# Buffers and banks for two units of a gated recurrence, and its low weight parts on VectorE

## The chip, the cores and the metric

One core of a Trainium2 chip runs the whole program. The metric is device time in microseconds (us); the kernel before was run three times, and one more execution was recorded with the hardware profiler. TensorE is called PE here, VectorE DVE, ScalarE ACT, GpSimd POOL and SyncE SP, as in the profile; PEld is the loading of weights into PE.

## The reference

The trunk has two layers on 1024 tokens of width 1024. The first layer mixes tokens with a gated linear recurrence (HGRN2), the second with latent attention; a causal convolution MLP follows each. The change is in the recurrence alone:

```python
def _hgrn2_mixer(h, w_in, lower_bound, out_norm, w_out):
    q, f, i, g = jnp.split(h @ w_in, 4, axis=-1)
    forget = lb + (1.0 - lb) * jax.nn.sigmoid(f)
    key_in = 1.0 - forget
    log_f = jnp.log(forget)
    o = _chunk_gated_recurrence(heads(jax.nn.silu(q)), heads(key_in), heads(i), heads(log_f))
    o = _rmsnorm(o, out_norm) * jax.nn.silu(heads(g))
    return o.reshape(B, S, D_MODEL) @ w_out
# S_t = diag(f_t) S_{t-1} + k_t v_t^T ;  o_t = S_t^T q_t   per head, 8 heads, key and value width 128
```

## The kernel before

Every product is made from fp32 data that is split into a high part (rounded by ACT, line 128, the tile `whi` or `vgh`) and a low part (what is left, a subtraction, line 131, the tile `wlo` or `vgl`). PE multiplies high by high, high by low and low by high (`acc3`, lines 147 to 149).

`hgrn` works in 16 units, one for each of 8 heads and each of two halves (`hf`) of 512 tokens. Each unit has two parts.

- `project` makes the forget gate `Fg` with the key `K` (line 364 on), the query `q` and its gated form `Q` (lines 373 to 376), each from 24 matmuls of 512 columns into a bank `ps_mm`; then the value `v` and the output gate `g` from 96 matmuls of 256 columns (tiles `vgh`, `vgl`).
- `recur` makes the decayed scores by doubling: a group of 8 small matmuls (line 406, tile `sc`) gives the scores of one level, then DVE scales half of `Q` (line 417) and POOL half of `K` (line 419) with running decays `tot` (line 422), and the next level follows; one group with `q`, six levels, then line 432. After them come the transposed key (`pT`, line 443, copied by ACT at line 445), the state updates (`pu`, line 456; line 461 on DVE), the output `po` (lines 451 and 453) and its norm (lines 465 to 471). `flip` transposes the finished output (line 478), splits it and sends it out.

`weights` fetches the four weight tiles of a head into a ring of two raw tiles and splits them. A head's set is made while an earlier head is still running. The last units are taken in the order (6,0), (7,0), (6,1), (7,1), so that weights are made ten times, four tiles each. After the units, `out_projection` multiplies all heads' outputs (`oall`), 192 matmuls for each half.

The code names one tile after another; a scheduler in the framework puts each engine's instructions in order ahead of time, by data, buffers (`bufs`) and banks. At run time each engine takes its own list strictly in that order. A tile with one buffer can't be written again before its last reader is done; a PSUM bank likewise. So the number of buffers decides how early the scheduler can place the work of a following unit.

Of the kernel before, what the change touches and what calls it, by code (L numbers as in the profile page):

```python
# [9 lines left out]
F32 = mybir.dt.float32  # L10
# [9 lines left out]
P = 128  # L20
D = 1024
S = 1024
HF = 512
# [7 lines left out]
LEVELS = (1, 2, 4, 8, 16, 32)  # L31
# [27 lines left out]
def trunk_kernel(ctx: ExitStack, tc: tile.TileContext, x, pos, par, gout, cst, msk, w_hin, w_hout,  # L59
                 w_min, w_qup, w_kvup, w_mout, w_up, w_down, out):  # L60
    nc = tc.nc
    pe, dve, act, pool = nc.tensor, nc.vector, nc.scalar, nc.gpsimd
# [6 lines left out]
    psg = ctx.enter_context(tc.tile_pool(name="psg", bufs=2, space=PSUM))  # L69
# [18 lines left out]
    def fetch_w(src):  # L88
        raw = wpool.tile([P, 1024], F32, tag="wraw", name="wraw", bufs=2)
        nc.sync.dma_start(out=raw, in_=src)  # L90
        return raw
# [41 lines left out]
    def load_w(src, tag="w", wp=None, bufs=3, eng=pool):  # L133
        lo_eng = dve if first else eng
        raw = first.pop(0) if first else fetch_w(src)
        hi = (wp or wpool).tile([P, 1024], F32R, tag=tag + "hi", name="whi", bufs=bufs)
        lo = (wp or wpool).tile([P, 1024], F32R, tag=tag + "lo", name="wlo", bufs=bufs)
        split(raw, hi, lo, lo_eng=lo_eng)
        return hi, lo

    def v3(ap, a):
        return ap.rearrange("p (a b) -> p a b", a=a)
# [178 lines left out]
    def hgrn(layer, h):  # L321
        with ExitStack() as st:
            tp = st.enter_context(tc.tile_pool(name="g_t", bufs=2))
            early = st.enter_context(tc.tile_pool(name="g_e", bufs=2))
            wv = st.enter_context(tc.tile_pool(name="g_wv", bufs=1))
            ps = st.enter_context(tc.tile_pool(name="g_ps", bufs=1, space=PSUM))
# [11 lines left out]
            wts = {}  # L338

            def weights(hd):  # L340
                wf = load_w(w_hin[8 + hd])
                wq = load_w(w_hin[hd])
                vgh = wv.tile([P, KD, 2 * P], F32R, tag="vgh", name="vgh")
                vgl = wv.tile([P, KD, 2 * P], F32R, tag="vgl", name="vgl")
                for i, src in enumerate((w_hin[16 + hd], w_hin[24 + hd])):
                    raw = vg_first.pop(0) if vg_first else fetch_w(src)
                    split(v3(raw, KD), vgh[:, :, i * P:(i + 1) * P], vgl[:, :, i * P:(i + 1) * P],
                          lo_eng=dve if vg_first else pool)
                wts[hd] = wf, wq, vgh, vgl

            def project(hd, hf, bank=ps_mm):
                wf, wq, vgh, vgl = wts[hd]
                hh, hl, rb, y = h[hf]

                def proj(w):
                    p = bank()
                    acc3(p, [(w[0][:, k * P:(k + 1) * P], w[1][:, k * P:(k + 1) * P], hh[:, k, :], hl[:, k, :])
                             for k in range(KD)])
                    return p

                pf = proj(wf)
                Fg = early.tile([P, HF], F32, tag="F", name="Fg")
                K = tp.tile([P, HF], F32, tag="K", name="K")
                dve.tensor_tensor(out=Fg, in0=pf, in1=rb, op=ALU.mult)
                act.activation(out=K, in_=Fg, func=AF.Sigmoid, scale=-1.0)
                act.activation(out=Fg, in_=Fg, func=AF.Sigmoid)
                pool.tensor_scalar(out=Fg, in0=Fg, scalar1=oml[:, hd:hd + 1], scalar2=lb[:, hd:hd + 1],
                                   op0=ALU.mult, op1=ALU.add)
                pool.tensor_scalar(out=K, in0=K, scalar1=oml[:, hd:hd + 1], scalar2=0.0, op0=ALU.mult, op1=ALU.add)
                pq = proj(wq)  # L370
                q = early.tile([P, HF], F32, tag="q", name="q", bufs=1)
                Q = tp.tile([P, HF], F32, tag="Q", name="Q")
                dve.tensor_tensor(out=q, in0=pq, in1=rb, op=ALU.mult)  # L373
                act.activation(out=Q, in_=q, func=AF.Sigmoid)
                dve.tensor_tensor(out=q, in0=q, in1=Q, op=ALU.mult)
                dve.tensor_tensor(out=Q, in0=q, in1=Fg, op=ALU.mult)

                v = tp.tile([P, 4, P], F32, tag="v", name="v")
                g = tp.tile([P, 4, P], F32, tag="g", name="g", bufs=3)
                for tt in range(2):  # L380
                    pv = ps_mm()
                    for t2 in range(2):
                        t = 2 * tt + t2
                        ts_ = slice(t * P, (t + 1) * P)
                        acc3(pv[:, t2 * 256:(t2 + 1) * 256],
                             [(hh[:, k, ts_], hl[:, k, ts_], vgh[:, k, :], vgl[:, k, :]) for k in range(KD)])
                    p3 = v3(pv, 2)
                    for t2 in range(2):
                        t = 2 * tt + t2
                        yt = y[:, t:t + 1]  # L390
                        act.activation(out=v[:, t, :], in_=p3[:, t2, 0:P], func=AF.Identity, scale=yt)
                        act.activation(out=g[:, t, :], in_=p3[:, t2, P:2 * P], func=AF.Sigmoid, scale=yt)
                        dve.scalar_tensor_tensor(out=g[:, t, :], in0=p3[:, t2, P:2 * P], scalar=yt, in1=g[:, t, :],  # L393
                                                 op0=ALU.mult, op1=ALU.mult)
                pool.tensor_tensor(out=g, in0=g, in1=goutb[:, None, :].broadcast_to([P, 4, P]), op=ALU.mult)
                return Fg, K, q, Q, v, g

            def recur(hd, hf, prj, state):
                Fg, K, q, Q, v, g = prj

                def scores(qq):
                    sc = ps.tile([P, 4, 64], F32, tag="sc", name="sc", bufs=2)
                    for c in range(4):
                        for b in range(2):
                            sl = slice(c * P + b * 64, c * P + b * 64 + 64)
                            pe.matmul(sc[b * 64:b * 64 + 64, c, :], lhsT=K[:, sl], rhs=qq[:, sl], start=True, stop=True)  # L406
                    return sc

                SD = tp.tile([P, 4, 64], F32, tag="SD", name="SD", bufs=1)
                dve.tensor_tensor(out=SD, in0=scores(q), in1=fold[:, None, 0:64].broadcast_to([P, 4, 64]), op=ALU.mult)  # L410

                def scale(tot, m):
                    nb = HF // (2 * m)
                    tv = tot.rearrange("p (b two) -> p b two", two=2)
                    Qv = Q.rearrange("p (b two m) -> p b two m", two=2, m=m)
                    Kv = K.rearrange("p (b two m) -> p b two m", two=2, m=m)
                    dve.tensor_tensor(out=Qv[:, :, 1, :], in0=Qv[:, :, 1, :],  # L417
                                      in1=tv[:, :, 0:1].broadcast_to([P, nb, m]), op=ALU.mult)
                    pool.tensor_tensor(out=Kv[:, :, 0, :], in0=Kv[:, :, 0, :],
                                       in1=tv[:, :, 1:2].broadcast_to([P, nb, m]), op=ALU.mult)  # L420
                    nt = tp.tile([P, nb], F32, tag=f"tot{m}", name=f"tot{m}", bufs=2 if m == 64 else 1)
                    dve.tensor_tensor(out=nt, in0=tv[:, :, 0], in1=tv[:, :, 1], op=ALU.mult)
                    return nt

                tot = Fg
                for li, m in enumerate(LEVELS):
                    sc = scores(Q)
                    tot = scale(tot, m)
                    dve.copy_predicated(SD, masks[:, li, None, :].broadcast_to([P, 4, 64]), sc)
                sc = ps.tile([P, 4, 64], F32, tag="sc", name="sc64", bufs=2)  # L430
                for c in range(4):
                    pe.matmul(sc[0:64, c, :], lhsT=K[:, c * P:c * P + 64], rhs=Q[:, c * P + 64:(c + 1) * P],
                              start=True, stop=True)
                ST = tp.tile([P, 4, P], F32, tag="ST", name="ST", bufs=1)
                pool.memset(ST[64:P, :, 0:64], 0.0)
                act.copy(out=ST[0:64, :, 0:64], in_=SD[0:64])
                act.copy(out=ST[64:P, :, 64:P], in_=SD[64:P])
                act.copy(out=ST[0:64, :, 64:P], in_=sc[0:64])
                tot = scale(tot, 64)
# [9 lines left out]
                for c in range(4):  # L449
                    first = state is None  # L450
                    pe.matmul(po[:, c, :], lhsT=ST[:, c, :], rhs=v[:, c, :], start=True, stop=first)
                    if not first:
# [33 lines left out]
            vg_first = []  # L486
# [6 lines left out]
            goutb = wv.tile([P, P], F32, tag="goutb", name="goutb")  # L493
            nc.sync.dma_start(out=goutb, in_=gout.partition_broadcast(P))
            nc.sync.dma_start(out=cs, in_=cst)
            mstage = tp.tile([P, len(LEVELS), 64], F32, tag="ST", name="mstage", bufs=1)
            nc.sync.dma_start(out=mstage, in_=msk)
            dve.tensor_copy(out=masks, in_=mstage)
            prj = project(0, 0, ps_wo)
# [549 lines left out]
```

## Time and profile before

| what | us |
|---|---|
| median of three runs | 2585.41 |
| lowest and highest of them | 2581.57, 2588.17 |
| the profiled execution | 2581.05 |
| its span, first to last instruction | 2579.2 |

The span is 1.85 us shorter than the profiled execution's own time. A row of a timeline gives the start, the duration, the engine, the line, the operation, the tiles as written<-read, and, in brackets, how long the engine had stood idle before it and who ended that. Durations of matmuls overlap, since they are pipelined: the difference between two starts tells what one costs.

### The profile page before, as it was taken

The numbers are of one execution on the slowest core, as the hardware profiler recorded it, in microseconds if no ns is written. First come the engines' busy times: TensorE is split into PE (matmuls) and PEld (weight loads), VectorE is DVE, ScalarE is ACT, GpSimd is POOL, SyncE is SP. The second block draws the span as 40 slices with busy tenths as digits, with TensorE's granted clock in tenths as the row PEclk, the third lists the DMA queues.
The fourth block names the chain that finished last, engine by engine and source line by source line (L and its number), as shares of the span: only waits on it lengthen the run. The fifth ranks groups of instructions, "written<-read, shape, count | busy, mean of one in ns | idle before, by whom it ended". The sixth has DMA issues, their size and how long they took to land.

```text
span 2579.2 us, 35799 instructions
## 1 busy us (share of the span) xinstructions
PE 2483.0 (96%) x13860; PEld 2069.2 (80%) x13860; DVE 1698.1 (66%) x3033; ACT 1080.6 (42%) x1777; POOL 392.5 (15%) x386
## 2 busy tenths in 40 slices
PE   7999999998999999999999999999999999999999
PEld 6888888876777778888888788888877787888887
DVE  8355555555788888774535777777578888875333
ACT  5322223322444444433433566656444444443322
POOL 3334445521100000000003323221000000000000
PEclk9999999999999999999999999989999999999999
DMA  3111111343433332264331000002543333226443
GB/s 138 42 50 50 50 50 66 113 144 121 154 120 111 108 112 89 90 230 155 128 126 50 17 34 33 34 26 103 200 155 120 109 110 111 91 91 220 155 170 116
DMA packets 88298, 270.18 MB, mean 105 GB/s; under 512 B 9920, under 2 KB 10304, under 8 KB 86976
## 3 DMA queue, kind: packets, MB, share of 16 engines
q1 hardware_dynamic: 88128, 267.90, 29.5%
q8 instruction: 109, 1.79, 0.3%
q14 instruction: 61, 0.50, 0.1%
HBM read 207.04 MB, written 60.82 MB: 104 GB/s over the span
## 4 chain that ended last, share of the span: by engine, by line
PE 86%; DVE 6%; ACT 3%; DMA 3%; issue 1%; SPq 0%; ACTq 0%; DVEq 0%
PE ps_mm L251 19%; PE ps_up L251 9%; PE ps_mm L147 8%; PE ps_mm L149 8%; PE ps_mm L148 7%; PE ps_up L942 7%; PE ps_mm L942 5%; PE ps_wo L942 5%; PE ps_wo L251 3%; PE sp L710 3%; PE ps_misc L942 2%; PE sc L406 2%; PE ps_misc L167 2%; DMA open_spill<-part 1%; PE ps_wo L739 1%
## 5 line engine op out<-in xcount | busy, mean ns | idle before, releaser
L128 ACT CAST whi<-wraw 128x1024 fp32r<-128x1024 f32 (+1 forms) x328 | 321.3, 993 | 579.2 <-PE ps_misc L942 236.6
L131 DVE TENSOR_TENSOR wlo<-wraw,whi 128x1024 fp32r<-128x1024 f32 (+1 forms) x298 | 337.9, 1146 | 286.3 <-ACT whi L128 285.9
L251 PE MATMUL ps_mm<-bop,whi 128*128 128x512 f32 x1536 | 477.7, 393 | 17.3 <-ACT x L888 9.5
L251 PEld LDWEIGHTS ps_mm<-bop,whi 128*128 128x128 f32 x1536 | 285.9, 188 | 89.8 <-ACT x L888 15.4
L251 PE MATMUL ps_mm<-bop,wlo 128*128 128x512 f32 x768 | 296.4, 391 | 0.9 <-DVE wlo L131 0.9
L862 DVE SCALAR_TENSOR_TENSOR x<-x,prm,x 128x1023 f32<-128x1023 f32 (+1 forms) x176 | 223.5, 1279 | 48.9 <-ACT x L859 47.9
L251 PE MATMUL ps_up<-bop,whi 128*128 128x512 f32 x704 | 220.7, 394 | 0.9 <-ACT whi L128 0.9
L251 PEld LDWEIGHTS ps_mm<-bop,wlo 128*128 128x128 f32 x768 | 144.2, 188 | 33.6 <-DVE wlo L131 2.2
L942 PE MATMUL ps_up<-ring,whi 128*128 128x512 f32 x528 | 159.9, 389 | 0.0
L251 PEld LDWEIGHTS ps_up<-bop,whi 128*128 128x128 f32 x704 | 131.8, 188 | 33.1 <-ACT whi L128 2.6
L417 DVE TENSOR_TENSOR Q<-Q,tot 128x256 f32<-128x256 f32 x96 | 65.6, 683 | 133.2 <-PE sc L406 105.3
L147 PE MATMUL ps_mm<-vgh,hh 128*128 128x256 f32 x512 | 146.0, 285 | 5.9 <-DVE q L373 5.6
L149 PE MATMUL ps_mm<-vgh,hl 128*128 128x256 f32 x512 | 145.4, 284 | 0.0
L148 PE MATMUL ps_mm<-vgl,hh 128*128 128x256 f32 x512 | 143.8, 281 | 0.0
L859 ACT ACTIVATE x<-x,prm 128x1024 f32<-128x1024 f32 x88 | 109.3, 1243 | 70.0 <-DVE x L886 48.2
L251 PE MATMUL ps_up<-bop,wlo 128*128 128x512 f32 x352 | 138.5, 394 | 0.0
L845 DVE TENSOR_TENSOR wraw<-wraw 128x512 f32<-128x512 f32 x176 | 120.8, 686 | 2.2
L147 PE MATMUL ps_mm<-hh,whi 128*128 128x512 f32 x288 | 115.7, 402 | 2.2 <-DVE g L393 1.2
L710 PE MATMUL sp<-kk,qq 128*128 128x256 f32 (+4 forms) x480 | 109.1, 363 | 8.7 <-ACT pp L725 8.5
L942 PEld LDWEIGHTS ps_up<-ring,whi 128*128 128x128 f32 x528 | 99.2, 188 | 20.7
L149 PE MATMUL ps_mm<-hh,wlo 128*128 128x512 f32 x288 | 115.5, 401 | 0.0
L888 ACT COPY x<-ps_mm 128x512 f32<-128x512 f32 x84 | 49.1, 584 | 153.0 <-PE ps_mm L251 153.0
(296 smaller groups left out, 5544.3 us busy)
## 6 DMA issues: line engine op xcount, KB each, us to landing
wraw<-in_w_up_dram SPq DMA_DIRECT2D x104, 512.0 KB, 3.7
wraw<-in_w_down_dram SPq DMA_DIRECT2D x88, 512.0 KB, 3.5
act_spill<-x SPq DMA_DIRECT2D x44, 512.0 KB, 2.6
araw<-act_spill SPq DMA_DIRECT2D x88, 256.0 KB, 3.6
wraw<-in_w_hin_dram SPq DMA_DIRECT2D x38, 512.0 KB, 3.5
oall<-o_spill SPq DMA_DIRECT2D x64, 256.0 KB, 4.6
o_spill<-oh SPq DMA_DIRECT2D x32, 256.0 KB, 2.0
o_spill<-ol SPq DMA_DIRECT2D x32, 256.0 KB, 2.2
```

What stands on the lines that cost most here:

```text
L128: act.copy(out=hi, in_=src)
L131: lo_eng.tensor_tensor(out=lo, in0=src, in1=hi.bitcast(F32), op=ALU.subtract)
L147: pe.matmul(ps, lhsT=lh, rhs=rh, start=(i == 0), stop=False)
L148: pe.matmul(ps, lhsT=lh, rhs=rl, start=False, stop=False)
L149: pe.matmul(ps, lhsT=ll, rhs=rh, start=False, stop=(i == n - 1))
L251: pe.matmul(p, lhsT=a[l][:, ks], rhs=b[:, r, k, :], start=first and k == 0 and n == 0, stop=k == KH - 1 and n == 2, skip_group_check=not f ...
L417: dve.tensor_tensor(out=Qv[:, :, 1, :], in0=Qv[:, :, 1, :], in1=tv[:, :, 0:1].broadcast_to([P, nb, m]), op=ALU.mult)
L710: pe.matmul(sp[:, 0:n], lhsT=qq[:, a, qs], rhs=kk[:, c, cl], start=(i == 0), stop=last)
L845: dve.tensor_tensor(out=o, in0=p, in1=q, op=op)
L859: act.activation(out=y, in_=u, func=AF.Identity, scale=cw(2, ff), bias=pcol("cb", layer * 44 + ff))
L862: dve.scalar_tensor_tensor(out=y[:, i:S], in0=u[:, 0:S - i], scalar=cw(2 - i, ff), in1=y[:, i:S], op0=ALU.mult, op1=ALU.add)
L942: pe.matmul(acc[d], lhsT=w[l][:, d * P:(d + 1) * P], rhs=a[:, r], start=j == 0 and n == 0, stop=j == NFF - 1 and n == 2)
```

## The change

In `hgrn` the tiles `Fg`, `K`, `Q` and `v` get three buffers in place of two; `SD`, `ST` and the decays `tot` get two in place of one. The score groups of line 406 leave the two banks that they shared with the transposed key, the state updates and the last group (line 432); they take the two banks of the tag `wo`, which this stage used once only. All low parts of the weights in this stage are formed by DVE; before, POOL formed 37 of 40.

```diff
             def weights(hd):
-                wf = load_w(w_hin[8 + hd])
-                wq = load_w(w_hin[hd])
+                wf = load_w(w_hin[8 + hd], eng=dve)
+                wq = load_w(w_hin[hd], eng=dve)
...
                     split(v3(raw, KD), vgh[:, :, i * P:(i + 1) * P], vgl[:, :, i * P:(i + 1) * P],
-                          lo_eng=dve if vg_first else pool)
+                          lo_eng=dve)
...
-                Fg = early.tile([P, HF], F32, tag="F", name="Fg")
-                K = tp.tile([P, HF], F32, tag="K", name="K")
+                Fg = early.tile([P, HF], F32, tag="F", name="Fg", bufs=3)
+                K = tp.tile([P, HF], F32, tag="K", name="K", bufs=3)
...
-                Q = tp.tile([P, HF], F32, tag="Q", name="Q")
+                Q = tp.tile([P, HF], F32, tag="Q", name="Q", bufs=3)
...
-                v = tp.tile([P, 4, P], F32, tag="v", name="v")
+                v = tp.tile([P, 4, P], F32, tag="v", name="v", bufs=3)
...
                 def scores(qq):
-                    sc = ps.tile([P, 4, 64], F32, tag="sc", name="sc", bufs=2)
+                    sc = psg.tile([P, 4, 64], F32, tag="wo", name="sc", padded_shape=[P, 8, 64])
...
-                SD = tp.tile([P, 4, 64], F32, tag="SD", name="SD", bufs=1)
+                SD = tp.tile([P, 4, 64], F32, tag="SD", name="SD", bufs=2)
...
-                    nt = tp.tile([P, nb], F32, tag=f"tot{m}", name=f"tot{m}", bufs=2 if m == 64 else 1)
+                    nt = tp.tile([P, nb], F32, tag=f"tot{m}", name=f"tot{m}", bufs=2)
...
-                ST = tp.tile([P, 4, P], F32, tag="ST", name="ST", bufs=1)
+                ST = tp.tile([P, 4, P], F32, tag="ST", name="ST", bufs=2)
```

The instructions are the same ones; their order within the recurrence stage is another, and 37 subtractions change engine. After that stage PE's order is the same but for a few rows.

**On PE, the end of a unit.** Here `pT` is the transposed key, `pu` a state update, `po` the output, and `sc<-q` the first score group of the unit that follows. In the kernel before, in the middle of the stage:

```order
L451 MATMUL po<-v,ST 128x128
L453 MATMUL po<-state,Q 128x128
L451 MATMUL po<-v,ST 128x128
L443 MATMUL pT<-ident,K 128x128 x4
L456 MATMUL pu<-v,K 128x128 x2
L453 MATMUL po<-state,Q 128x128
L451 MATMUL po<-v,ST 128x128
L456 MATMUL pu<-v,K 128x128
L453 MATMUL po<-state,Q 128x128
L451 MATMUL po<-v,ST 128x128
L406 MATMUL sc<-q,K 64x64 x8
```

The same place in the changed kernel:

```order
L406 MATMUL sc<-q,K 64x64 x4
L451 MATMUL po<-v,ST 128x128 x2
L443 MATMUL pT<-ident,K 128x128 x4
L406 MATMUL sc<-q,K 64x64 x4
L406 MATMUL sc<-Q,K 64x64 x8
L147 MATMUL ps_mm<-hh,whi 128x512
L148 MATMUL ps_mm<-hl,whi 128x512
L149 MATMUL ps_mm<-hh,wlo 128x512
```

The next unit's first two score groups have moved ahead of the state updates, and 24 matmuls of the projection stand between `pT` and the first `pu`; before, `pu` came directly behind `pT`.

**On DVE, after a unit's first score group.** `SD` is the first scores masked, `vgl` and `wlo` are low parts of weights, `Q` is scaled by the decays. The changed kernel:

```order
L410 TENSOR_TENSOR SD<-sc,fold 128x256
L131 TENSOR_TENSOR vgl<-wraw,vgh 128x8x128
L417 TENSOR_TENSOR Q<-Q,Fg 128x256
L429 COPY_PREDICATED SD<-masks,sc 128x256
L131 TENSOR_TENSOR vgl<-wraw,vgh 128x8x128
L393 SCALAR_TENSOR_TENSOR g<-ps_mm,st_y,g 128x128
L131 TENSOR_TENSOR wlo<-wraw,whi 128x1024
L364 TENSOR_TENSOR Fg<-ps_mm,rb 128x512
L461 SCALAR_TENSOR_TENSOR state<-state,tot_2026,pu 128x128
L417 TENSOR_TENSOR Q<-Q,tot_2291 128x128x2
```

Three subtractions of line 131 stand in DVE's list around two scalings of `Q`, two of them between the scalings; before, POOL did them.

**On PE, the end of the stage.** `oall` are the finished heads. The kernel before:

```order
L432 MATMUL sc_6003<-Q,K 64x64 x4
L451 MATMUL po<-v,ST 128x128
L453 MATMUL po<-state,Q 128x128
L451 MATMUL po<-v,ST 128x128
L443 MATMUL pT<-ident,K 128x128 x4
L456 MATMUL pu<-v,K 128x128 x2
L453 MATMUL po<-state,Q 128x128
L451 MATMUL po<-v,ST 128x128
L456 MATMUL pu<-v,K 128x128
L453 MATMUL po<-state,Q 128x128
L451 MATMUL po<-v,ST 128x128
L453 MATMUL po<-state,Q 128x128
```

The `flip` (line 478) of the last unit follows directly. The changed kernel, the last `po` of the last unit and what follows it:

```order
L148 MATMUL ps_mm<-oall,whi 128x512
L453 MATMUL po<-state,Q 128x128
L149 MATMUL ps_mm<-oall,wlo 128x512
L147 MATMUL ps_mm<-oall,whi 128x512
L148 MATMUL ps_mm<-oall,whi 128x512
```

Of the output projection, 25 matmuls now stand between that `po` and the `flip`, and 18 to 22 at most earlier steps of this last unit's end; before they stood ahead of it, between its score groups.

## Rows read from the trace of the kernel before

**Rows 1.** The page, span and busy time of PE and PEld (share, instructions).
```profile
span 2579.2 us, 35799 instructions
PE 2483.0 (96%) x13860; PEld 2069.2 (80%) x13860; DVE 1698.1 (66%) x3033; ACT 1080.6 (42%) x1777; POOL 392.5 (15%) x386
```

**Rows 2.** Busy time by stage: start:end length, engines, PEclk, DMA share, GB/s.
```profile
47.00:632.00 585.00, 549.46 (x4764) 471.85 (x4759) 310.93 (x826) 166.71 (x435) 225.82 (x209) 0.99 0.22 74
632.00:700.00 68.00, 64.53 (x277) 52.18 (x278) 45.18 (x68) 27.14 (x33) 7.81 (x3) 0.97 0.43 151
```

**Rows 3.** The same for one head, its two units: PE, PEld, DVE, ACT, POOL.
```profile
222.53:290.91 68.38, 65.30 (x588) 56.55 (x588) 36.13 (x99) 18.91 (x53) 27.33 (x27) 1.00 0.13 47
```

**Rows 4.** Waits of PE from 47 to 632 us: total, times, longest.
```profile
PE pu L456 <- ACT K L445: 9.5, 13, 0.7
PE ps_mm L147 <- DVE q L373: 5.6, 13, 0.7
PE ps_misc L478 <- DVE g L471: 4.5, 1, 4.5
PE po L451 <- ACT ST L438: 4.1, 9, 0.5
PE ps_mm L147 <- DMA oall<-o_spill: 2.1, 1, 2.1
...
PE po L453 <- DVE state L461: 1.3, 6, 0.2
```

**Rows 5.** Timeline of PE around score groups, one alone and two together.
```profile
227.09 0.69 PE L406 MATMUL sc<-q,K 128*64 128x64 f32 x16
227.61 0.64 PE L406 MATMUL sc<-Q,K 128*64 128x64 f32 x16
...
231.60 0.28 PE L148 MATMUL ps_mm<-vgl,hh 128*128 128x256 f32 x1
231.81 0.69 PE L406 MATMUL sc<-Q,K 128*64 128x64 f32 x16
232.42 0.39 PE L149 MATMUL ps_mm<-vgh,hl 128*128 128x256 f32 x1
232.65 0.28 PE L147 MATMUL ps_mm<-vgh,hh 128*128 128x256 f32 x1
232.77 0.28 PE L148 MATMUL ps_mm<-vgl,hh 128*128 128x256 f32 x1
```

**Rows 6.** The low parts' subtractions, 47 to 632 us: busy, mean ns | idle before.
```profile
L131 POOL TENSOR_TENSOR vgl<-wraw,vgh 128x1024 fp32r<-128x1024 f32 x18 | 43.1, 2403 | 26.1 <-ACT vgh L128 26.0
L131 POOL TENSOR_TENSOR wlo<-wraw,whi 128x1024 fp32r<-128x1024 f32 x16 | 38.4, 2398 | 16.0 <-ACT whi L128 15.5 <-POOL ST L435 0.5
L131 DVE TENSOR_TENSOR wlo<-wraw,whi 128x1024 fp32r<-128x1024 f32 x11 | 14.2, 1288 | 4.3 <-ACT whi L128 4.3
```

**Rows 7.** Timelines of DVE and POOL: scalings of one level, free and beside a subtraction.
```profile
316.15 0.42 DVE L417 TENSOR_TENSOR Q<-Q,tot 128x256 f32<-128x256 f32 x1 [3.79 <-PE sc L406]
316.26 0.80 POOL L419 TENSOR_TENSOR K<-K,tot 128x256 f32<-128x256 f32 x1 [1.29 <-PE sc L406]
...
347.39 2.39 POOL L131 TENSOR_TENSOR wlo<-wraw,whi 128x1024 fp32r<-128x1024 f32 x1 [1.10 <-ACT whi L128]
347.70 2.36 DVE L417 TENSOR_TENSOR Q<-Q,tot 128x256 f32<-128x256 f32 x1 [1.97 <-PE sc L406]
```

**Rows 8.** Timelines of SP and ACT: a weight load's issue and its cast.
```profile
341.94 0.38 SPq L90 DMA_DIRECT2D wraw<-in_w_hin_dram  x1
...
346.27 1.05 ACT L128 CAST whi<-wraw 128x1024 fp32r<-128x1024 f32 x1 [4.77 <-DMA wraw<-in_w_hin_dram]
```

**Rows 9.** Timeline of PE at the end of the stage.
```profile
620.88 0.49 PE L453 MATMUL po<-state,Q 128*128 128x128 f32 x2
625.92 1.25 PE L478 MATMUL ps_misc<-ident,g 128*128 128x128 f32 x4 [4.54 <-DVE g L471]
...
632.61 1.22 PE L147 MATMUL ps_mm<-oall,whi 128*128 128x512 f32 x2 [2.18 <-DMA oall<-o_spill]
```

More of the change, by code (lines that the diff above doesn't have):

```diff
@@ L495, in hgrn @@
             nc.sync.dma_start(out=cs, in_=cst)
-            mstage = tp.tile([P, len(LEVELS), 64], F32, tag="ST", name="mstage", bufs=1)
+            mstage = tp.tile([P, len(LEVELS), 64], F32, tag="ST", name="mstage", bufs=2)
             nc.sync.dma_start(out=mstage, in_=msk)
```

## Prediction

> **What bounds the kernel now.** I read the page first. PE is busy for 96% of the span and no other engine for more than 66% [rows 1], so a change on another engine counts only where PE waits for it. The windows by stage come next: in the recurrence, from 47 to 632 us, PE is busy for 549.46 of 585.00 us [rows 2], so 35.5 us there are idle. This is the first limit of what a better overlap of units can give. The windows of one head show the same in the small: 65.30 of 68.38 us [rows 3], or 3.1 us idle a head, while DVE is busy for 36.13 us and POOL for 27.33 us.
>
> A busy PE need not be a PE at its peak, so I looked at starts. Matmuls of 256 columns follow each other at 0.12 us (232.65 and 232.77), and a group of scores stands between them without a pause [rows 5]. Inside the busy time there is no hidden slack that an earlier start of something would take away. What can go is the idle time, and the list of waits says what it is [rows 4]: the copy of the transposed key (9.5 us in 13 waits), the bank that DVE frees by reading `q` (5.6 us in 13), the copy of the scores (4.1 us), the states (1.3 us), the last unit's norm (4.5 us, once) and a load of finished heads (2.1 us). The smaller rest of the list lies mostly in the start of the stage.
>
> **The change part by part.** *Units in flight.* The order shows where PE's waits go. Between `pT` and the first `pu` there was nothing in most units; now in steady units 19 to 24 projection matmuls of 512 columns stand there, over 4 us for a wait of 0.7 us. Ahead of `po` stand 8 to 17 matmuls of 256 columns and score groups of the next unit, about 1 to 2 us for a wait of 0.5. The wait for the bank of `q` arose since `v` and `g` matmuls followed at once behind the first scores; now projection matmuls of 512 columns stand there. The first `po` that needs a state has 13 or more such matmuls ahead of it. The last norm is waited for over 25 matmuls of the output projection; one of 512 columns is estimated at 0.23 us (twice the columns at the same rate), so 5.7 us cover the 5.04 us from the start of the last `po` at 620.88 to the flip at 625.92 [rows 9]. I take these five waits as gone: 9.5 + 5.6 + 4.1 + 1.3 + 4.5 = 25.0 us. The load of `oall` stays, since the output still goes to memory and back behind the flip, and so does the start. The bounds are 0 and the whole 35.5 us.
>
> *Cut groups.* The number of matmuls is the same, but the score groups are cut and spread more. I counted in the orders how often PE goes from another kind of matmul to a score matmul: 103 times before, 140 after. A separate group of 8 costs more than 8 that follow others. Alone: from 231.60 to 232.65 lie 1.05 us for two matmuls of 0.12 us and the group, so the group takes 0.81 us. Behind another: 227.61 - 227.09 = 0.52 us [rows 5]. The difference is 0.29 us an entry, and 37 more of them cost 10.7 us. Many new entries lie beside `po`, `pu` and the flips rather than beside projections, for which I have no such pair of rows; the price could be nothing there. I take the full 10.7, as these rows are the nearest, and keep 0 as the lower end.
>
> *The subtractions.* POOL loses 37 at 2.40 us, DVE gets them at 1.29 us, its own mean for such a tile [rows 6]: 47.7 us more on DVE, four a head or 5.2 us. DVE has 32 us free a head [rows 3]. What hides them is PE's own work within a score step: after a group's end DVE's scaling took 0.42 us and POOL's 0.80, ended at 317.06, some 1.0 us after the group [rows 7]; in the new order the usual step has 25 matmuls of 256 columns, 2.95 us at 0.118. That leaves about 2 us, more than one subtraction. Price on the path: 0. Without the cover, each would cost 1.29 us, 47.7 us in all. The end below nothing is closed: freeing POOL shortens scalings that no PE wait of any weight stands behind [rows 4].
>
> There is a give-back on DVE that costs nothing to have. At 347.39 POOL subtracts for 2.39 us and DVE's scaling beside it, issued at 347.70, lasts 2.36 us in place of 0.42 [rows 7]: DVE stands still until POOL is through. [...]
>
> *A new wait in DVE's list.* DVE takes its list in order, and a `wlo` now stands ahead of the next `Fg`, a state and a scaling. It waits for ACT's cast, which waits for a load that starts only when a `vgl` has freed its raw tile. From issue at 341.94 to the cast at 346.27 are 4.33 us [rows 8]; with the cast of 1.05 and the subtraction of 1.29 that is 6.7 us from release to release of DVE. Ahead of the score group that needs the scaling behind it stand 24 projection matmuls, a split score group, then 13 more and state updates: about 5.5 + 1.3 + 4.8 = 11.6 us by rates of 0.23 us a matmul. I cost it at 0, with a reserve of about 2 us after the other DVE work in between, and keep it for the slower side.
>
> **Sum.** 2581.05 - 25.0 + 10.7 = 2566.8 us on the profiled execution's own time. That execution lies 4.4 us under the median of the three runs, so the forecast for the median is 2585.41 - 14.3 = 2571 us.
>
> **The rivals.** *The cuts are cheap and the clock helps.* If entries beside `po` and `pu` cost nothing, the gain is 25; the end of the stage adds up to 2 us, since the granted clock is 0.97 over the 68 us after it [rows 2] and PE would stand still for less long before. Time 2585 - 27 = 2558. For it: the new entries are mostly of that kind. Against it: an entry changes the shape of the matmul there as well.
>
> *Waits change their names.* PE's five waits go, but the chain of a unit is the same length, and new ones arise at the cut groups or behind subtractions; half of the 25 us comes back: 2585.4 - 12.5 + 10.7 = 2584, no change. For it: DVE's list is longer by 5.2 us a head. Against it: a cover of about 2 us in each step.
>
> *The late weight stops the recurrence (slower).* Where the load takes longer than in rows 8 by more than the reserve of 2 us, each further us stands in PE ten times, once for each set of weights. It decides at 14.3 / 10 = 1.4 us beyond the reserve, a load-to-cast time of about 7.8 us. At 9 us it is 2585.4 - 14.3 + 10 x 2.7 = 2598. For it: in the last units every unit brings a new set of weights and the loads share the queue with outputs. Against it: the row shows 4.33 us.
>
> *Far more is gained.* PEld is busy for 56.55 of 68.38 us a head [rows 3]; if that were PE's true load, 11.8 us a head lay open, 94 us over eight heads, 2491 us. Against it speak the starts [rows 5]: in the stretch of 256-column matmuls nothing is open. [...]
>
> **How the numbers follow.** Times within 0.3% of the median, 7.8 us, are about what a measurement of this kernel can't tell from no change. The forecast (2571, with its own range 2566 to 2576 for half of the cut groups' price either way) gets 0.54, cheap cuts 0.16, far more 0.02, waits that change names 0.17, the late weight 0.11. So faster 0.72, same 0.17, slower 0.11. The range leaves out the far gain at the low end and most of the late weight at the high end: 2558 to 2586.
>
> **What would show it.** Right: the waits of PE for `K` of line 445, `q` of line 373, `ST` and the last `g` gone or below 1 us each in total, PE's idle time in the stage near 10 us, a head's two units at 66 to 67 us rather than 68.4, DVE's scalings of `Q` near 0.42 us in the mean, and POOL without line 131 in this stage. Wrong: waits of PE's score groups for `Q` or `K`, or of `po` for the state, of more than 5 us in total; DVE idle before line 131 for ACT's cast with PE idle at the same time; or a head that takes no less than before though its waits are gone, by which the cut groups would cost more than 0.29 us each. Stages after 700 us should keep their length, as their order stays.

## Result: 1.1% faster, a little beyond the range's lower end

Median of the changed kernel 2555.99 us (four runs, 2554.16 to 2558.56) against 2583.53 us for the kernel before beside it (2581.57 to 2588.17): a ratio of 0.9892, 95% interval 0.9874 to 0.9909, 27.5 us gained. Timed once more, it was 2553.87 against 2584.82, ratio 0.9877 (0.9860 to 0.9893). The forecast was 2571, the range 2558 to 2586. The sign and the place are those of the forecast; the gain is about twice as large.

The page of the changed kernel, its span and busy time, for [rows 1]:

```profile
span 2552.4 us, 35685 instructions
...
PE 2487.1 (97%) x13860; PEld 2079.8 (81%) x13860; DVE 1708.1 (67%) x3070; ACT 1088.2 (43%) x1777; POOL 307.7 (12%) x349
```

PE does as much as before, 2487.1 us against 2483.0, in a span that is 26.8 us shorter. The windows by stage and of one head (two units), for [rows 2, 3]:

```profile
47.00:632.00 585.00, 576.38 (x4850) 500.08 (x4849) 345.78 (x883) 187.79 (x450) 155.95 (x177) 0.99 0.23 79
...
170.40:236.10 65.70, 65.70 (x589) 57.53 (x588) 37.02 (x102) 20.15 (x53) 18.77 (x22) 1.00 0.14 49
```

Of 585 us only 8.6 are idle on PE, where 35.5 were (the same window, of which the stage now fills some 28 us less), and a head takes 65.70 us instead of 68.38 with no idle time at all. PE's waits in the same stretch, for [rows 4]:

```profile
PE ps_mm L147 <- DMA oall<-o_spill: 2.9, 1, 2.9
PE ps_misc L199 <- DVE dg L191: 1.7, 1, 1.7
PE ps_misc L167 <- DVE ol L131: 1.4, 1, 1.4
PE sc L406 <- DVE Q L417: 1.2, 1, 1.2
PE sc L406 <- DVE st_z L156: 1.1, 1, 1.1
PE ps_mm L147 <- DVE Fg L364: 0.3, 1, 0.3
```

All five waits that the forecast took as gone are gone, and what is new is small. The load of `oall` stayed, as forecast. The timeline of PE shows what took their place: the two halves of a score group stand around `po` and `pT` without a pause, and at the stage's end (for [rows 9]) the last `flip` comes without a wait:

```profile
203.59 0.45 PE L406 MATMUL sc<-q,K 128*64 128x64 f32 x8
203.97 0.71 PE L451 MATMUL po<-v,ST 128*128 128x128 f32 x4
204.52 0.60 PE L443 MATMUL pT<-ident,K 128*128 128x128 f32 x4
205.05 0.45 PE L406 MATMUL sc<-q,K 128*64 128x64 f32 x8
205.33 0.64 PE L406 MATMUL sc<-Q,K 128*64 128x64 f32 x16
205.89 0.50 PE L147 MATMUL ps_mm<-hh,whi 128*128 128x512 f32 x1
...
591.88 0.38 PE L453 MATMUL po<-state,Q 128*128 128x128 f32 x2
...
597.81 0.60 PE L478 MATMUL ps_misc<-ident,g 128*128 128x128 f32 x4
```

On DVE, the lines of the stage (busy, mean ns | idle before), the first from the kernel before and the others from the changed one, for [rows 6, 7]:

```profile
L417 DVE TENSOR_TENSOR Q<-Q,tot 128x256 f32<-128x256 f32 x96 | 65.6, 683 | 133.2 <-PE sc L406 105.3 <-PE sc L432 26.9
...
L417 DVE TENSOR_TENSOR Q<-Q,tot 128x256 f32<-128x256 f32 x96 | 47.2, 492 | 52.7 <-PE sc L432 36.2 <-PE sc L406 15.4
L131 DVE TENSOR_TENSOR wlo<-wraw,whi 128x1024 fp32r<-128x1024 f32 x33 | 40.8, 1237 | 19.8 <-ACT whi L128 19.8
L131 DVE TENSOR_TENSOR vgl<-wraw,vgh 128x1024 fp32r<-128x1024 f32 x18 | 23.9, 1328 | 0.4 <-ACT vgh L128 0.3
```

`Q` is scaled faster than before, and DVE now waits 19.8 us for ACT's casts ahead of `wlo`, the wait that the forecast named. PE's list shows only one wait for `Q`, of 1.2 us.

**Where the gain arose.** The first matmul of the feed-forward part (line 251) marks the end of the recurrence stage with its output projections. It starts at 670.6 us before and at 641.5 us after: 29.1 us gained. What follows takes 1908.7 us before and 1910.9 after, so 2.3 us are lost again there, at a mean granted clock of 0.98 instead of 0.99. Line 251 and the window up to it (PE's busy time is its third number), each before and after:

```profile
L251 PE MATMUL ps_mm<-bop,whi x134: 388/389/499, 670.6 to 722.0; 128*128 128x512 f32 x134
0.00:670.58 670.58, 622.80 (x5119) 532.43 (x5119) 376.25 (x923) 213.67 (x505) 248.21 (x231) 0.99 0.24 83
...
L251 PE MATMUL ps_mm<-bop,whi x178: 388/389/504, 641.5 to 721.7; 128*128 128x512 f32 x178
0.00:641.46 641.46, 622.61 (x5118) 539.24 (x5119) 387.42 (x960) 221.23 (x505) 163.59 (x194) 0.99 0.25 87
```

PE is busy for 622.8 us before and 622.6 after. By busy time, then, the whole gain is idle time that went, and the 37 more cut groups of the forecast seem to cost nothing. The experiments show that this reading misleads.

### The profile page after: what moved, and what is told of

It is laid out like the page before. It is cut to its first block, busy times and chain, and to the rows that moved or that the text cites. A ratio compares the mean times of both kernels' runs of the same rounds, so it can differ in the third digit from the quotient of the medians.

```text
span 2552.4 us, 35685 instructions
## 1 busy us (share of the span) xinstructions
PE 2487.1 (97%) x13860; PEld 2079.8 (81%) x13860; DVE 1708.1 (67%) x3070; ACT 1088.2 (43%) x1777; POOL 307.7 (12%) x349
## 4 chain that ended last, share of the span: by engine, by line
PE 89%; DVE 5%; ACT 3%; DMA 1%; issue 1%; SPq 0%; ACTq 0%; DVEq 0%
PE ps_mm L251 20%; PE ps_up L251 9%; PE ps_mm L147 8%; PE ps_mm L148 8%; PE ps_mm L149 8%; PE ps_up L942 7%; PE ps_mm L942 5%; PE ps_wo L942 5%; PE sc L406 3%; PE ps_wo L251 3%; PE sp L710 3%; PE ps_misc L942 2%; PE ps_misc L167 2%; PE ps_wo L739 1%; PE ps_misc L752 1%
## 5 line engine op out<-in xcount | busy, mean ns | idle before, releaser
L131 DVE TENSOR_TENSOR wlo<-wraw,whi 128x1024 fp32r<-128x1024 f32 (+1 forms) x316 | 359.3, 1148 | 302.8 <-ACT whi L128 302.5
L148 PE MATMUL ps_mm<-hl,whi 128*128 128x512 f32 x288 | 113.6, 394 | 0.0
```

What stands on the lines that cost most here:

```text
L131: lo_eng.tensor_tensor(out=lo, in0=src, in1=hi.bitcast(F32), op=ALU.subtract)
L148: pe.matmul(ps, lhsT=lh, rhs=rl, start=False, stop=False)
```

## Experiments

Theory A: the gain comes from PE's order alone; a wait costs more than its idle row, and a cut group costs what the forecast said, so that the two errors are hidden in PE's busy time. Rival B: POOL's subtractions moved to DVE carry a part. Rival C: cuts are free and a wait costs its idle row. Of the parts, theory A left open whether the bank or the buffers make the order.

| run | median us | before beside it | ratio, 95% interval | line 251 starts at |
|---|---|---|---|---|
| e1_pool_subs | 2550.33 | 2584.40 | 0.9871 (0.9856 to 0.9886) | 638.3 |
| e2_dve_subs_only | 2580.92 | 2584.40 | 0.9990 (0.9979 to 1.0001) | 668.4 |
| e3_bank_only | 2554.36 | 2584.40 | 0.9884 (0.9871 to 0.9898) | 642.3 |
| e4_buffers_only | 2627.48 | 2584.40 | 1.0158 (1.0138 to 1.0178) | 719.7 |
| a1_after_again | 2553.87 | 2584.82 | 0.9877 (0.9860 to 0.9893) | 642.3 |
| e5_bank_dve_subs | 2553.18 | 2584.82 | 0.9876 (0.9858 to 0.9893) | 640.0 |
| b1_direct_output | 2554.15 | 2584.82 | 0.9873 (0.9854 to 0.9893) | 637.8 |

**e1_pool_subs**, the changed kernel without its first part:

```diff
-                wf = load_w(w_hin[8 + hd], eng=dve)
-                wq = load_w(w_hin[hd], eng=dve)
+                wf = load_w(w_hin[8 + hd])
+                wq = load_w(w_hin[hd])
...
-                          lo_eng=dve)
+                          lo_eng=dve if vg_first else pool)
```

> The change with its subtractions back on POOL: buffers and the score bank alone. By theory A (the gain is the five waits that the new order covers, each worth more than its idle row) the order keeps every wait covered and has 131 cut groups against 140, so the ratio to before is about 0.990, 24 to 27 us gained, and only the about 2 us at the first score group stay lost. By rival B (the subtractions' move carries a part, since POOL's work holds up DVE) at most 20 us are gained, ratio above 0.992, and PE waits for Q or K in the stage by more than 5 us.

34 us gained, more than either theory said; in the whole stage PE's score groups wait 0.6 us for `Q` and not at all for `K`. B falls: without the move nothing is lost.

**e2_dve_subs_only**, the kernel before with that part alone (the same lines, the other way round).

> The kernel before with the subtractions on DVE alone: PE's order is nearly that of before (102 cut groups, 103 before). Theory A: the five waits stay, the gain is 0 to 3 us (the first score group of the stage comes about 2 us earlier), ratio 0.999 to 1.000. Rival B: 6 us or more are gained, ratio below 0.998.

3.5 us at the medians, with an interval that reaches 1. In the profile the first score group starts at 44.5 us instead of 46.6 and the rest of the stage keeps its length; all five waits are there. This is the ratio that A named, with a gain a little above its 0 to 3 us.

**e3_bank_only**, the kernel before with one line:

```diff
-                    sc = ps.tile([P, 4, 64], F32, tag="sc", name="sc", bufs=2)
+                    sc = psg.tile([P, 4, 64], F32, tag="wo", name="sc", padded_shape=[P, 8, 64])
```

> Only the score groups' bank moved; buffers and subtractions as before. The order already puts 19 or more matmuls between pT and pu in every unit and has 132 cut groups. Theory A: what counts is PE's order, so 20 to 26 us are gained, ratio 0.990 to 0.992, with new waits of at most 5 us for single buffers. Rival (the second and third buffers are needed for it): under 14 us, with waits of PE for copies or scalings held up by SD, ST or tot.

30 us gained, the changed kernel's whole gain and above the 20 to 26 expected. The only new waits are 1.4 us for `Q` and 0.7 us for the last `g`. So the second and third buffers aren't needed for it.

**e4_buffers_only**, the changed kernel with the bank and the subtractions as before (the line of e3 and those of e1, taken back).

> Only the buffers are more; the score bank and the subtractions as before. The order covers pT in 11 of 16 units and the copy of the scores in most, with 103 cut groups as before, so no cut is paid for here. Theory A (a wait costs its whole start-to-start gap, 0.89 us at pT against 0.73 idle): 10 to 14 us gained, ratio 0.995 to 0.996. Rival C (a wait costs its idle row and no more): 7 to 9 us. If the stage gains as much per wait as the change did with its cuts, cuts are free.

Wrong for both theories: 43 us slower at the medians, 49.5 us in the profiled executions that follow. PE's waits in the stage, with those of over 5 us in total:

```profile
PE ps_misc L478 <- DVE g L471: 15.0, 5, 4.6
PE sc L406 <- POOL K L419: 14.9, 16, 1.1
...
PE pu L456 <- ACT K L445: 7.8, 5, 2.2
PE sc L432 <- POOL K L419: 7.3, 7, 1.1
```

With more buffers but scores, `pT` and `pu` still taking turns in two banks, the order covers some waits on the copy and opens others: PE waits 22.2 us, in 23 times, for POOL's scaling of `K` between score groups. Up to line 251 PE is idle for 72.6 us (719.71 less 647.12 busy), 24.8 more than before. The other half of the loss is in the busy time, 647.1 against 622.8 us, and the granted clock is 0.94 there against 0.99. The timeline shows one such place:

```profile
376.24 0.69 PE L406 MATMUL sc<-Q,K 128*64 128x64 f32 x16
377.94 0.69 PE L406 MATMUL sc<-Q,K 128*64 128x64 f32 x16 [1.01 <-POOL K L419]
379.63 1.12 PE L432 MATMUL sc<-Q,K 128*64 128x64 f32 x8 [1.00 <-POOL K L419]
380.68 0.58 PE L147 MATMUL ps_mm<-vgh,hh 128*128 128x256 f32 x1
381.06 0.42 PE L148 MATMUL ps_mm<-vgl,hh 128*128 128x256 f32 x1
381.27 0.41 PE L149 MATMUL ps_mm<-vgh,hl 128*128 128x256 f32 x1
```

Behind two idle times of 1.0 us with one score group between them, matmuls of 256 columns start 0.21 us apart instead of 0.12: the granted clock is 0.50, and some 2 us later the starts draw together again (0.15 us from 382.76 to 382.91). What brings the clock down is not shown, and it doesn't fall behind every such pair. The same pair stands at 229.18 and 230.88 in this trace, and the clock stays at 1.00 (the last lines are the windows behind the pair above and behind this one):

```profile
229.18 0.69 PE L406 MATMUL sc<-Q,K 128*64 128x64 f32 x16 [1.01 <-POOL K L419]
230.88 0.68 PE L432 MATMUL sc<-Q,K 128*64 128x64 f32 x8 [1.01 <-POOL K L419]
...
380.70:382.70 2.00, 2.00 (x10) 2.00 (x10) 0.59 (x2) 0.36 (x1) 0.79 (x1) 0.50 0.00 0
231.50:233.50 2.00, 2.00 (x18) 2.00 (x18) 0.59 (x2) 0.41 (x2) 0.79 (x1) 1.00 0.00 0
```

**a1_after_again, e5_bank_dve_subs, b1_direct_output.** The changed kernel once more; the bank and the subtractions without the buffers (e3 with the first part of the change); and e1 with the last unit's output multiplied straight from its two tiles:

```diff
-            put_out(*pend[:2], flip(pend[2]))
+            last = flip(pend[2])
...
-            out_projection(1, w_hout)
+            out_projection(1, w_hout, last)
```

> The changed kernel once more, beside the two below on one chip: 0.989 to 0.990. Theory A as it stands after the first four runs: 3 to 5 us slower than with POOL's subtractions.

> Score bank and DVE subtractions, buffers as before. If the bank alone carries the gain, 0.987 to 0.990, 27 to 32 us gained, and the buffers are worth 4 us at most either way. If DVE's subtractions cost because DVE gets late, PE should show waits for Q, K or ST of some us here.

> Buffers and bank with the subtractions on POOL, and the last unit's output taken straight from its two tiles instead of through memory. PE's wait for the load (3.0 us) should go and 1 to 2 us of a wait for the flip's split stay: 1 to 3 us better than the same kernel without it, ratio to before about 0.986. Rival: another wait of the same length stands there, 0.987.

a1 came out at 0.9877, a larger gain than expected, and A's 3 to 5 us between it and e1 are not shown: the intervals overlap. e5 gains as much as the change, 31.6 us, with no wait of PE for `Q`, `K` or `ST` but one of 1.2 us, so the buffers add nothing that these runs resolve, and neither does the engine of the subtractions: the intervals of e1, e3, e5 and the change overlap. b1 didn't beat e1. The load's wait is gone, but at 619.67 PE waits 2.70 us for a bank that DVE still has to read, so the rival named there held; and what follows line 251 takes 1916.8 us instead of e1's 1907.9. The mean granted clock of the profiled executions differs, 0.985 against 0.987, and b1's four executions go with it, from 2545.93 us at a mean of 0.989 to 2556.37 at 0.985; that the clock is the whole cause isn't shown. No version tried is faster than the change by more than the intervals.

**m1_prices**, the disputed prices by themselves. The order is written out; V are 24 matmuls of 256 columns, s a score group, tr `pT` with ACT's copy, u `pu`:

```python
for _ in range(N): V(24); s(); s()
for _ in range(N): V(12); s(); V(12); s()
...
for _ in range(N): V(24); s(); s(); o()
for _ in range(N): V(24); s(); o(); s()
for r in range(N): tr(r % 2); V(24); u(r % 2)
for r in range(N): V(12, pu); V(12, pT[0]); tr(0); u(0)
```

> No model here: eight stretches of eight periods each, with the kernel's own shapes (its output is not the reference's, so its total time says nothing). Between each pair of stretches only the order of the same matmuls differs. Cut price, two groups of 8 scores behind 24 matmuls of 256 columns against one group behind each 12: the forecast's price and theory A say 0.25 to 0.30 us more a period, rival C (cuts are free) under 0.05. Beside 128x128 matmuls (scores, scores, po against scores, po, scores): A leaves open 0 to 0.3. Wait price, pT, copy by ACT, pu at once against 24 matmuls of 256 columns between them: theory A says that the period grows by 0.15 us or more beyond the idle row of that wait (0.73 idle, 0.89 in all); C says by the idle row and no more.

The timeline, in order: two groups together, the two cut apart, the copy covered, the copy waited for.

```profile
43.99 1.15 PE L64 MATMUL sc<-Q,K 128*64 128x64 f32 x32
45.07 3.13 PE L52 MATMUL pv<-hh 128*128 128x256 f32 x24
48.14 1.15 PE L64 MATMUL sc<-Q,K 128*64 128x64 f32 x32
...
61.00 1.70 PE L52 MATMUL pv<-hh 128*128 128x256 f32 x12
62.62 0.69 PE L64 MATMUL sc<-Q,K 128*64 128x64 f32 x16
63.24 1.70 PE L52 MATMUL pv<-hh 128*128 128x256 f32 x12
64.86 0.69 PE L64 MATMUL sc<-Q,K 128*64 128x64 f32 x16
65.48 1.70 PE L52 MATMUL pv<-hh 128*128 128x256 f32 x12
...
264.24 0.60 PE L72 MATMUL pT<-ident,K 128*128 128x128 f32 x4
267.55 1.06 PE L77 MATMUL pu<-v,kT 128*128 128x128 f32 x8
268.44 0.60 PE L72 MATMUL pT<-ident,K 128*128 128x128 f32 x4
...
302.67 0.60 PE L72 MATMUL pT<-ident,K 128*128 128x128 f32 x4
304.00 1.16 PE L77 MATMUL pu<-v,kT 128*128 128x128 f32 x8 [0.73 <-ACT kT L73]
...
307.86 0.60 PE L72 MATMUL pT<-ident,K 128*128 128x128 f32 x4
```

A period takes 4.15 us with the groups together (43.99 to 48.14) and 4.48 cut (61.00 to 65.48): a cut costs 0.33 us. Beside `po` it is 0.35 (periods of 5.04 and 5.39), beside matmuls of 512 columns 0.37. These are above the 0.25 to 0.30 and the 0 to 0.3 expected. Cuts aren't free, and C falls there. The period with the copy covered is 4.20 us (264.24 to 268.44), waited for 5.19 (302.67 to 307.86): the wait costs 0.99 us where its row says 0.73. C falls here too.

**m2_wait_prices**, the other waits in the order of the kernel before. Only operands differ between stretches: `Y` is `ST` or a constant, `X` the copy or a constant, `a`, `b`, `d` states still being made or a constant:

```python
V(24); # the last score group and the copy into ST
po(0, Y[:, 0, :], v[:, 0, :]); po(0, Y[:, 0, :], st[3]); po(1, Y[:, 0, :], v[:, 1, :])
# pT and its copy
u(0, v[:, 0, :], 0); u(1, v[:, 1, :], 1); po(1, X[:, 1, :], a); po(2, X[:, 2, :], b)
u(2, b, 2); po(2, X[:, 2, :], d); po(2, X[:, 3, :], d); s(sc[0], X, d); s(sc[1], X, d)
```

> No model here either (its output is not the reference's). Five stretches of eight periods; a period is 24 matmuls of 256 columns and then the tail of a unit in the order of the kernel before: the last score group, po, pT, pu, po with the states, two score groups. The order of PE is the same in all five; only what the matmuls read differs: nothing that is still being made, the copy of pT alone, the copy of the scores (ST) alone, the states alone, all three. What a wait costs is a period less the first stretch's period. Theory A: pT's copy costs 0.9 to 1.0 us against an idle row of 0.73, ST 0.15 us or more above its idle row, the states 0.4 to 0.7 us a period against idle rows of 0.1 to 0.3, and the three add up to 1.9 to 2.4 us. C: each costs its idle row and no more, 1.3 to 1.5 us in all.

PE's waits (each of the three is in two stretches of eight periods):

```profile
PE pu L96 <- ACT kT L90: 11.6, 16, 0.7
PE T L74 <- DVE st L97: 10.6, 32, 0.4
...
PE T L74 <- ACT ST L82: 7.1, 16, 0.5
```

| reads what is being made | period us | costs | idle row a period |
|---|---|---|---|
| nothing | 7.62 | | |
| pT's copy | 8.62 | 1.00 | 11.6 / 16 = 0.73 |
| ST | 8.19 | 0.57 | 7.1 / 16 = 0.44 |
| states (two waits) | 8.84 | 1.22 | 10.6 / 16 = 0.66 |
| all three | 10.42 | 2.80 | 1.83 |

Periods of a stretch agree within 0.02 us (but for the first two of the first, of which some work is moved ahead); in the last the usual one is given, since three of its seven were longer (10.46 to 11.44). The prices add up (2.79), and they are 1.3 to 1.8 times the idle rows, above even A's 2.4 for the three: the states cost far more than its 0.4 to 0.7 us, while `ST` stands 0.13 us above its row, a little under the 0.15 expected. A reason can be read in m1's rows: four `pT` are drawn 0.60 us long, but the next matmul can start 0.36 us after their first (268.44 to V at 268.80 in that trace). The other 0.24 us of the drawn time are no time that the next matmul has to wait, and PE's idle time is counted only behind them (302.67 + 0.60 + 0.73 = 304.00).

## Why the prediction fell short

**Right.** The five waits are gone and none of their size took their place; "waits change their names" and "the late weight stops the recurrence" didn't come. The subtractions cost and bring nothing that the times resolve (e1 against the change, e2 against before), as priced. DVE's scalings of `Q` fell from 683 ns in the mean to 492 ns, not quite the 0.42 us named, and POOL has no line 131 left in the stage. A head came out at 65.70 us, below the 66 to 67 named.

**The step that failed** is the term "I take these five waits as gone: 9.5 + 5.6 + 4.1 + 1.3 + 4.5 = 25.0 us", and under it the sentences "Inside the busy time there is no hidden slack" and "What can go is the idle time". The mechanism was right; the term was mis-sized, since I added idle rows where I should have taken starts. Two rows of the kernel before have it:

```profile
257.32 0.60 PE L443 MATMUL pT<-ident,K 128*128 128x128 f32 x4
258.65 0.71 PE L456 MATMUL pu<-v,K 128*128 128x128 f32 x4 [0.73 <-ACT K L445]
```

From start to start these are 1.33 us; four `pT` with nothing to wait for behind them take 0.36 us in m1. Measured as starts, against the interval of the same kinds of matmul where nothing is waited for, the kernel before loses 11.6 us at the copy (13 times 1.00 less 0.11). Another 1.3 come with it, since the matmul behind each waited `pu` starts 0.21 us after it in place of 0.11: 12.9 in all, and 13.0 by m2's price. It loses 6.5 at the bank of `q`, 4.7 at `ST`, 6.4 at the states (35 steps from `pu` to `po` at 0.236 us in place of 0.111, and 56 between `po` at 0.152 in place of 0.115), 4.7 at the last norm: 35.2 us. The states are the largest error, 6.4 for a row of 1.3: seven of their 13 idle times are of 0.13 us, too short for the list, and the start behind each waited `po` comes late as well. Another 2.0 us came at the start, which the forecast took to stay (the first score group at 44.58 instead of 46.55), which e2 shows to be the subtractions' doing.

**The cuts** were priced at 0.29 us an entry, and by themselves they cost 0.33 to 0.37. The kernels confirm the price. In the traces, with the groups of line 432 counted too, PE goes from another kind of matmul to a score matmul 119 times before and 152 times after, 33 more. Up to line 251 all kernels run the same matmuls, so each interval between two starts can be compared with the same two kinds where nothing is waited for and the granted clock is 1.00. By this estimate the matmuls by themselves take 10.3 us more in the change than before, 0.31 for each cut, against the forecast's 10.7 in all; in e1 4.3 us for 15 more cuts, in e3 8.9 for 24. What lies above these intervals, waits and the stretches at a granted clock of 0.50 (17.1 us long before, 13.7 after) together, is 56.3 us before and 17.0 after: 39.3 us less, of which the list above names 35.2 and 2.0.

**The sum as it should have been:** 2581.05 - 39.3 + 10.3 + 2.3 (lost behind the stage) = 2554.4 on the profiled execution's own time, which was 2554.16; the forecast had 25.0 and 10.7. The 39.3 and 10.3 are estimates from the traces, good to about 1 us, and their difference, 29.0, is the measured gain up to line 251 within 0.1 us. So the price of the cuts held and that of the waits was some 14 us too small. "The cuts are cheap and the clock helps" came nearest in time, but by luck: the cuts weren't cheap, and behind the stage 2.3 us were lost. "Far more is gained" stays refuted: the head has no idle time left at 65.70 us, with PEld at 57.53, and PEld alone doesn't fill it.

I also took the change as one thing. The order was mine to read, and the runs show what makes it: one line, the bank (e3). The buffers without it cost 43 us.

## What to carry to other kernels

Price a PE wait from start to start against the same two matmuls without a wait, not by the idle time in front of it (0.99 us for a row of 0.73 in m1), take in the start behind it, and look for waits too short to be listed. Where two matmuls on a dependent chain share banks with independent work, separate the banks before adding buffers: buffers alone can give an order that waits more (in e4 72.6 us of idle time on PE up to line 251, in the kernel before 47.8). Try the parts of such a change apart, since here one line of twelve was the gain.

## What the runs showed of the hardware

In e4 the granted clock was 0.50 behind two idle times of 1.0 us with one score group between them (starts 0.21 us apart) and 1.00 behind the same pair elsewhere; in that kernel the loss in busy time, 24.3 us, is as large as that in idle time, 24.8. In the kernel before, waits of up to 0.73 us left the clock at 1.00 in the head of [rows 3]; behind the wait of 4.54 us [rows 9] it was 0.50 from 625.8 to 636.0 us. Moving about 48 us of subtractions (at DVE's 1.29 us each) from POOL, beside which one of DVE's scalings lasted 2.36 us in place of 0.42 [rows 7], to DVE changed the time by no more than the intervals (e2: 0.9979 to 1.0001).
